# Gate weights of four mLSTM heads folded in four large VectorE instructions, their loads moved earlier, and the heads written one step apart

## The chip, the cores and the metric

The kernel runs on one core of a Trainium2 chip. The metric is the time of one execution on the device in microseconds (us), and each kernel is timed several times. PE is the matmul engine (TensorE), PEld its weight loads, DVE is VectorE, ACT is ScalarE, POOL is GpSimd, and SP is SyncE, which here only issues loads.

## The reference, cut to what matters

Two layers over 256 tokens of 1024 channels: an mLSTM block (4 heads of 512 channels), then a sparse attention block. The change lies in the first part of the mLSTM block.

```
x_in, z = split(rmsnorm(x, g) @ w_in, 2)            # 256 x 2048 each
x_conv  = silu(conv4(x_in) + conv_b)                # 4 taps along the tokens
q, k    = headwise(x_conv, w_q), headwise(x_conv, w_k)   # 4 x 4 blocks
v       = headwise(x_in, w_v)
gates   = concat([q, k, v]) @ w_if + b_if           # 6144 -> 8
h       = mlstm(q, k, v, input gate, forget gate)   # per head, causal, stabilised
out     = ((layernorm(h) * ln_w + skip * x_conv) * silu(z)) @ w_out
```

Since q, k and v are blockwise products, the gates can be computed from x_conv and x_in with *folded* gate weights, w_q and w_k (and w_v) multiplied into w_if. Folding is a product with a broadcast and a sum over the 4 (or 8) inner rows.

## The kernel before, in words

Weights come from HBM in **units** of 1 MB, each in two halves of 512 KB. `load_unit` (L258) issues a half from SP into one of 4 raw buffers `wr`. ACT rounds it to `wh` (L274). The remainder `wl` is made in one of two ways: DVE subtracts (L280), or ACT writes the negated copy (L277) and POOL issues an accumulating transfer `wl<-wr` that adds the raw half (L278). The list `BY_DMA` says which. `wh` and `wl` have 5 buffers each, and two units are loaded ahead (`LOOK`).

`project_channels` (L402) multiplies one unit with the input: 48 matmuls (L411), 16 k-blocks by channels with three products each (two of `wh`, one of `wl`). By `LAG` the products of `wl` stand 4 steps later, so the last 8 matmuls of a unit need the remainder of its second half. Its result lies in a PSUM bank, `px` (2 buffers) or `acc1` (1), until DVE has scaled it by the row scale `rb1` into `xin` (L438). `rb1` comes from `norm1` (L384): sums of squares, two small matmuls (L388), POOL's power (L325), two matmuls (L378) and a copy (L389).

Units 0 to 7 are x_in of the four heads, two each; 8 to 15 are z; 16 to 23 are the output projection (L694). The loop over heads (L431) does for each head h, in the order of the text: two units; block-diagonal matrices of the head's 4 x 4 blocks by POOL (`bdq`, `bdv`, L398); the head's part of the folded gate weights (`gate_weights`, L461: a product L463 and a sum L464, once for v into the last 8 columns of `bdv`, once for q and k into those of `q`); the convolution `xc` on ACT, POOL and DVE (L476 to L487); Silu (L489); the products with the block-diagonal matrices (v by L504, q by L497) and the scores (L511, L512). The gate weights `wif` (768 KB), the constants `cst` (228 KB) and x itself (1 MB, for the residual) are loaded by SP after the first unit's evacuation: a one-element copy from `rb1` into each tile (L441 to L448) makes those loads wait for it.

The order on each engine is not that of the text. A scheduler places the instructions by its own model of their times; each engine then runs its list in order, and a waiting instruction holds what stands behind it on its engine.

Of the kernel before, what the change touches and what calls it, by code (L numbers as in the profile page):

```python
# [202 lines left out]
def trunk(ctx, tc, a, out, dbg=None):  # L203
# [77 lines left out]
            halves.append((hi, lo))  # L281
        return halves

    plan = [(a["wi1"], i, KT, 256) for i in range(16)] + [(a["wo1"], i, 4, 512) for i in range(8)]
    of_step = {"v": [(a["wi2v"], i, 4, 280) for i in range(4)], "c": [(a["wi2"], i, 4, 512) for i in range(2)]}
    for j, step in enumerate(("k", "q0", "q1")):
        of_step[step] = [(a["wi2k"], i, KT, 256) for i in (2 * j, 2 * j + 1)]
# [140 lines left out]
        GP.memset(t, 0.0)  # L428
    xcs, vs1, scs = [], [], []
    convw = CA("convw").rearrange("p (t c) -> p t c", t=4)  # L430
    for h in range(NH):  # L431
        xin = T([P, 4, S + 3], tag="xin", bufs=2)
        GP.memset(xin[:, :, 0:3], 0.0)
        for u in range(2):
            def evac_x(ps, x_=xin[:, 2 * u:2 * u + 2, 3:], first=(h, u) == (0, 0)):
                if first:
                    norm1()
                V.tensor_tensor(x_, ps, spread(rb1), op=OP.mult)  # L438
            project_channels(a["wi1"], 2 * h + u, evac_x, ("px", "px", "acc1")[(2 * h + u) % 3])
            if (h, u) == (0, 0):  # L440
                V.tensor_copy(cst[:, 0:1], rb1[:, 0:1])  # L441
                nc.sync.dma_start(cst, a["cst"][:, 0:n_res])
                wifs = [T([P, 16, n // 128, 8], tag="zt", bufs=ZT, name="wif") for n in (1024, 512)]
                for t, o_, n in zip(wifs, (0, 1024), (1024, 512)):
                    V.tensor_copy(t[:, 0, 0, 0:1], rb1[:, 0:1])
                    nc.sync.dma_start(t.rearrange("p a b c -> p (a b c)"), a["wif"][:, o_:o_ + n])
                for i in range(2):
                    V.tensor_copy(xt[i][:, 0, 0:1], rb1[:, 0:1])  # L448
                    nc.sync.dma_start(xt[i], a["x"][:, i * 512:(i + 1) * 512].rearrange("(t p) c -> p t c", p=P))
        if h == 0:  # L450

            wqk = CA("wqk").rearrange("p (c i) -> p c i", c=16)
            wv = CA("wv").rearrange("p (c i) -> p c i", c=16)
            atmp = T([P, 16, 4, 4], tag="f4", bufs=F4, name="atmp")
            V.tensor_tensor(atmp, CA("wkrep").rearrange("p (c i j) -> p c i j", c=16, i=4),
                            wqk[:, :, 0:4, None].to_broadcast([P, 16, 4, 4]), op=OP.mult)
            AT = T([P, 16, 4], name="AT")
            V.tensor_reduce(AT, atmp.rearrange("p c i j -> p c j i"), axis=AX.X, op=OP.add)
        own = slice(4 * h, 4 * h + 4)

        def gate_weights(out, wgt, wif, nq):  # L461
            tmp = T([P, 4, nq * 4, 8], tag="wtmp", bufs=2)
            V.tensor_tensor(tmp, wif[:, own, :, :], wgt[:, own, :, None].to_broadcast([P, 4, nq * 4, 8]), op=OP.mult)  # L463
            V.tensor_reduce(out, tmp.rearrange("p c i g -> p c g i"), axis=AX.X, op=OP.add)  # L464

        bdq = blockdiag(AT[:, own, :], F32)
        bdv = blockdiag(wv[:, 4 * h:4 * h + 4, :], F32, PG)
        gate_weights(bdv[:, :, P:PG], wv, wifs[1], 1)
        xc = T([P, 4, S], tag="f4", bufs=F4, name="xc")
        tap_w = lambda tap, c: convw[:, tap, 4 * h + c:4 * h + c + 1]  # L470
        if h in CB_:
            x1 = T([P, 4, S], tag=XT, bufs={"zt": ZT, "sc2": 1}[XT], name="x1")
        for c in range(4):
            cbias = CA("convb")[:, 4 * h + c:4 * h + c + 1]
            if h in CA_ or h in CB_:
                A.activation(xc[:, c, :], xin[:, c, 0:S], AF.Identity, scale=tap_w(0, c), bias=cbias)  # L476
            else:
                V.tensor_scalar(xc[:, c, :], xin[:, c, 0:S], tap_w(0, c), cbias, op0=OP.mult, op1=OP.add)
            if h in CB_:
# [12 lines left out]
        gate_weights(q[:, :, S:SG], wqk, wifs[0], 2)
        for c2 in range(2):
            ps = PS((P, 2, S))
            for c in range(2):
                k = 2 * c2 + c
                PE.matmul(ps[:, c, :], bdq[:, k, :], xc[:, k, :], start=True, stop=True)  # L497
            A.activation(q[:, 2 * c2:2 * c2 + 2, 0:S], ps, AF.Copy)
        v = T([P, 2, 4, PG], tag="f4", bufs=F4, name="v")
        rest = PS((P, 2, PG), tag="acc0")  # L500
        for tb in range(2):
            ps = PS((P, 3, PG), tag="pt")
            for c in range(4):
# [12 lines left out]
        V.tensor_tensor(gsc, gsc, ps[:, P:P + 2 * PG].rearrange("p (t n) -> p t n", t=2)[:, :, P:PG], op=OP.add)  # L516
        xcs.append(xc)
        vs1.append(v)
        scs.append(sc)

    ident_r = TS([P, P], F32R, name="ident_r")
    V.tensor_copy(ident_r, ident)
    maskt_r = T([P, 2, P], F32R, name="maskt_r")
    V.tensor_copy(maskt_r, C("maskt")[:, None, :].to_broadcast([P, 2, P]))
    causal = C("mask2")

    vsps = []
# [116 lines left out]
    lnw = CA("lnw")  # L644
    ys = []
    for h in range(NH):
        z = T([P, 4, S], tag="zt", bufs=ZT, name="z")
        for u in range(2):
# [72 lines left out]
    def after_block(n, tb, cols):  # L721
        squares(ss2, n, tb)

    nc.sync.dma_start(pkb, a["pkb"])
    gain2 = CB("g")

    def before_unit(n, kq):
# [416 lines left out]
```

## Time and profile before

| | |
|---|---|
| median of 3 runs | 381.38 us (380.86 to 384.1) |
| the profiled execution | 378.87 us, of which its span 377.1 us |
| mean granted PE clock | 0.984 |
| busy in the span | PE 350.6, DVE 255.7, ACT 241.5, POOL 134.7 us |

The span is from the first to the last instruction; 1.8 us lie around it. Busy times of engines overlap. PE is busy nearly throughout, so what PE waits for, and where, is what counts.

### The profile page before, as it was taken

What the parts mean: (1) busy time and instruction counts of PE and PEld (TensorE: products, weight loads), DVE (VectorE), ACT (ScalarE), POOL (GpSimd) and SP (SyncE); (2) the same over time, 40 slices, a digit from 0 to 9 for tenths busy, and PEclk for the clock granted to TensorE, in tenths of its full rate; (3) what the DMA queues carried; (4) which work ended last, traced back from release to release, by engine and by line L of the source; (5) the groups of instructions that cost most, each with busy time, mean ns of one, the idle gap of its engine ahead of it and who ended that gap; (6) DMA issues with size and microseconds to landing.
All of it is one profiled execution on the core that took longest, in us unless ns stands there. A gap on an engine that the chain in (4) does not pass through costs nothing.

```text
span 377.1 us, 6621 instructions
## 1 busy us (share of the span) xinstructions
PE 350.6 (93%) x2399; PEld 313.8 (83%) x2399; DVE 255.7 (68%) x535; ACT 241.5 (64%) x438; POOL 134.7 (36%) x165
## 2 busy tenths in 40 slices
PE   6998799979999979999999799999879999999991
PEld 6998799869998968988887699999869996777771
DVE  5976999756476548983243736687979789684515
ACT  6674669738468649765653744372579789996304
POOL 5226377433301124610100303283430283857003
PEclk9999899999999999999999999999989999999997
DMA  7889758765646978999998897546577865020003
GB/s 260 280 269 315 209 129 217 188 152 125 167 157 159 197 210 217 228 233 296 239 262 239 266 343 216 173 104 155 154 195 209 246 237 158 2 56 2 2 0 112
DMA packets 21633, 69.57 MB, mean 185 GB/s; under 512 B 2528, under 2 KB 2912, under 8 KB 21600
## 3 DMA queue, kind: packets, MB, share of 16 engines
q1 hardware_dynamic: 15472, 48.71, 38.7%
q0 software_dynamic: 4752, 16.83, 24.6%
q10 hardware_dynamic: 1376, 3.61, 2.9%
q8 instruction: 19, 0.31, 0.3%
q14 instruction: 14, 0.11, 0.1%
HBM read 50.87 MB, written 1.05 MB: 138 GB/s over the span
## 4 chain that ended last, share of the span: by engine, by line
PE 39%; DMA 23%; DVE 18%; issue 8%; ACT 8%; POOL 1%; SPq 1%; ACTq 0%; POOLq 0%; DVEq 0%
PE ps L411 17%; DMA wl<-wr 7%; DMA wr<-in_wo_dram 6%; DVE xc L487 6%; PE ps L694 6%; DVE wl L280 4%; DMA wr<-in_wi2z_dram 3%; DMA wr<-in_wi2k_dram 2%; ACT wh L274 2%; PE ps L984 2%; PE ps L909 2%; PE ps L897 2%; DMA cst<-in_cst_dram 2%; DMA xch<-in_xt_dram 1%; ACT wl L277 1%
## 5 line engine op out<-in xcount | busy, mean ns | idle before, releaser
L411 PE MATMUL ps<-hT,wh 128*128 128x256 f32 x832 | 139.5, 293 | 2.4 <-DVE hT L343 1.3
L274 ACT ACTIVATE wh<-wr 128x1024 fp32r<-128x1024 f32 (+2 forms) x90 | 89.5, 1000 | 58.1 <-PE ps L411 21.5
L411 PEld LDWEIGHTS ps<-hT,wh 128*128 128x128 f32 x832 | 121.8, 198 | 4.6 <-DVE hT L343 1.9
L280 DVE TENSOR_TENSOR wl<-wr,wh 128x1024 fp32r<-128x1024 f32 (+2 forms) x57 | 70.9, 1244 | 36.0 <-ACT wh L274 33.2
L411 PE MATMUL ps<-hT,wl 128*128 128x256 f32 x416 | 87.7, 287 | 0.0
L411 PEld LDWEIGHTS ps<-hT,wl 128*128 128x128 f32 x416 | 66.4, 193 | 1.0 <-issue 0.6
L278 POOL DMA_DIRECT2D wl<-wr x33 | 28.7, 877 | 107.9 <-ACT wl L277 103.5
L277 ACT ACTIVATE wl<-wr 128x1024 fp32r<-128x1024 f32 (+1 forms) x33 | 33.8, 1025 | 13.4 <-PE ps L694 6.6
L694 PE MATMUL ps<-wh,r 128*128 128x512 f32 x128 | 41.4, 398 | 0.0
L487 DVE SCALAR_TENSOR_TENSOR xc<-xin,pka,xc 128x256 f32<-128x256 f32 x44 | 30.8, 754 | 0.1
L694 PEld LDWEIGHTS ps<-wh,r 128*128 128x128 f32 x128 | 24.0, 188 | 5.5
L694 PE MATMUL ps<-wl,r 128*128 128x512 f32 x64 | 25.3, 395 | 0.0
L694 PE MATMUL ps<-wh,y 128*128 128x512 f32 x64 | 21.8, 406 | 0.0
L803 POOL TENSOR_TENSOR swap<-swap,trig 128x512 f32<-128x512 f32 x6 | 10.2, 1697 | 18.9 <-DMA swap<-qu 7.3
L775 PE MATMUL ps<-wl,hT 128*128 128x280 f32 (+1 forms) x48 | 15.8, 330 | 1.2 <-DMA wl<-wr 1.2
L846 PE MATMUL ps<-ka,qt 128*128 128x256 f32 (+1 forms) x32 | 12.0, 380 | 3.8 <-DVE nm L852 3.7
L774 PE MATMUL ps<-wh,hT 128*128 128x280 f32 (+1 forms) x48 | 15.5, 329 | 0.0
L776 PE MATMUL ps<-wh,hT 128*128 128x280 f32 (+1 forms) x48 | 15.2, 325 | 0.0
L694 PEld LDWEIGHTS ps<-wh,y 128*128 128x128 f32 x64 | 11.8, 188 | 3.1 <-issue 0.8
L694 PEld LDWEIGHTS ps<-wl,r 128*128 128x128 f32 x64 | 12.0, 188 | 2.8 <-DMA wl<-wr 0.2
L641 POOL TENSOR_TENSOR xc<-xc,pka 128x1024 f32<-128x1024 f32 x4 | 9.8, 2455 | 12.2 <-PE ps L512 12.2
L504 PE MATMUL ps<-m,xin 128*128 128x136 f32 x64 | 9.7, 299 | 3.6 <-DVE m L464 3.5
(473 smaller groups left out, 676.0 us busy)
## 6 DMA issues: line engine op xcount, KB each, us to landing
wr<-in_wi_dram SPq DMA_DIRECT2D x34, 512.0 KB
wl<-wr POOLq DMA_DIRECT2D x31, 512.0 KB, 5.9
wr<-in_wo_dram SPq DMA_DIRECT2D x24, 512.0 KB
wr<-in_wi2k_dram SPq DMA_DIRECT2D x12, 512.0 KB
wr<-in_wi2z_dram SPq DMA_DIRECT2D x8, 512.0 KB
wr<-in_wi2v_dram SPq DMA_DIRECT2D x8, 280.0 KB
cw<-in_cw_dram ACTq DMA_DIRECT2D x4, 512.0 KB
xch<-in_xt_dram SPq DMA_DIRECT2D x4, 256.0 KB
```

The costliest lines, as they stand in the source:

```text
L274: A.activation(hi[:, k, :], raw[:, k, :], AF.Copy)
L277: A.activation(lo[:, k, :], raw[:, k, :], AF.Copy, scale=-1.0)
L278: GP.dma_start(out=lo[:, k, :].rearrange("p k n -> p (k n)"), in_=raw[:, k, :].rearrange("p k n -> p (k n)"), accum_op=OP.add)
L280: V.tensor_tensor(lo[:, k, :], raw[:, k, :], f32(hi[:, k, :]), op=OP.subtract)
L411: PE.matmul(ps[:, c, :], w, (hl if i == 1 else hh)[:, k, :], start=(k, c, i) == (0, 0, 0), stop=(k, i) == (KT - 1, 2), skip_group_check=True)
L487: V.scalar_tensor_tensor(xc[:, c, :], xin[:, c, tap:tap + S], tap_w(tap, c), xc[:, c, :], op0=OP.mult, op1=OP.add)
L694: PE.matmul(acc, l, r[:, k % 2, cols], start=first and i == 0, stop=last and i == 2)
L774: PE.matmul(o_, lh, hi[:, k % 2, :], start=kt == 0, stop=False)
L775: PE.matmul(o_, lh, lo[:, k % 2, :], start=False, stop=False)
L776: PE.matmul(o_, ll, hi[:, k % 2, :], start=False, stop=kt == KT - 1)
L803: (GP, V)[RE[1]].tensor_tensor(sw, sw, turn(1), op=OP.mult)
L846: PE.matmul(o_, lq, ka[:, g, :, 0:w_], start=True, stop=False)
```

## The change

- The loads of `cst` and `wif` wait for the sum of squares (`sq1`) and no longer for `rb1`; the load of x and of `pkb` (140 KB, before it was among the first loads) waits for the first evacuation of head 2 (`XTH`).
- The folding for all heads is done once (`fold`): two products (128x512 and 128x1024) and two sums, in place of eight products and eight sums. For each head POOL copies 128x32 out of the result into `bdv` and `q`.
- The text of the head loop is split in two, `heads_x` (units) and `heads_products` (the rest), and written in the order A0 A1 B0 A2 B1 A3 B2 B3.
- Two casts, `ident_r` and `maskt_r`, go from DVE to POOL.
- `silu_z1` and the stages "Z" are written down and not used.

```diff
+    def heads_x(h):
+        xin = xins[h] = T([P, 4, S + 3], tag="xin", bufs=2)
...
             project_channels(a["wi1"], 2 * h + u, evac_x, ("px", "px", "acc1")[(2 * h + u) % 3])
             if (h, u) == (0, 0):
-                V.tensor_copy(cst[:, 0:1], rb1[:, 0:1])
-                nc.sync.dma_start(cst, a["cst"][:, 0:n_res])
...
+                small_weights()
+        if h == XTH:
+            V.tensor_copy(pkb[:, 0:1], xin[:, 0, 3:4])
+            nc.sync.dma_start(pkb, a["pkb"])
...
+    def small_weights():
+        wifs = [T([P, 16, n // 128, 8], tag="zt", bufs=ZT, name="wif") for n in (1024, 512)]
+        V.tensor_copy(cst[:, 0:1], sq1[:, 0, 0:1])
+        for t, o_, n in zip(wifs, (0, 1024), (1024, 512)):
+            V.tensor_copy(t[:, 0, 0, 0:1], sq1[:, 0, 0:1])
+            nc.sync.dma_start(t.rearrange("p a b c -> p (a b c)"), a["wif"][:, o_:o_ + n])
+        nc.sync.dma_start(cst, a["cst"][:, 0:n_res])
...
+        def gate_weights(wgt, wif, nq, name):
+            out = T([P, 16, 8], name=name)
+            tmp = T([P, 16, nq * 4, 8], tag="f4", bufs=F4, name="wtmp")
+            V.tensor_tensor(tmp, wif, wgt[:, :, :, None].to_broadcast([P, 16, nq * 4, 8]), op=OP.mult)
+            V.tensor_reduce(out, tmp.rearrange("p c i g -> p c g i"), axis=AX.X, op=OP.add)
+            return out
+        folded.update(AT=AT, wv=wv, gv=gate_weights(wv, wifs[1], 1, "gwv"), gq=gate_weights(wqk, wifs[0], 2, "gwq"))
...
-        gate_weights(bdv[:, :, P:PG], wv, wifs[1], 1)
+        GP.tensor_copy(bdv[:, :, P:PG], folded["gv"][:, own, :])
...
-        gate_weights(q[:, :, S:SG], wqk, wifs[0], 2)
+        GP.tensor_copy(q[:, :, S:SG], folded["gq"][:, own, :])
...
+    for stage in STAGES.split():
+        {"A": heads_x, "B": heads_products, "Z": silu_z1}[stage[0]](int(stage[1]))
+
     ident_r = TS([P, P], F32R, name="ident_r")
-    V.tensor_copy(ident_r, ident)
+    GP.tensor_copy(ident_r, ident)
     maskt_r = T([P, 2, P], F32R, name="maskt_r")
-    V.tensor_copy(maskt_r, C("maskt")[:, None, :].to_broadcast([P, 2, P]))
+    GP.tensor_copy(maskt_r, C("maskt")[:, None, :].to_broadcast([P, 2, P]))
```

What the scheduler makes of it stands at three places. First **DVE**, before, from the third evacuation on (`ps_402` is unit 2, `xc_325` head 0, `m` a block-diagonal matrix):

```order
L438 TENSOR_TENSOR xin_387<-ps_402,rb_29_153 128x2x256
L524 CAST maskt_r_971<-cst_70 128x256
L487 SCALAR_TENSOR_TENSOR xc_325<-xin_159,pka_71,xc_325 128x256 x4
L463 TENSOR_TENSOR wtmp_322<-wif_242,pka_71 128x128
L463 TENSOR_TENSOR wtmp_347<-wif_241,pka_71 128x256
L464 TENSOR_REDUCE m_58_320<-wtmp_322 128x4x8
L464 TENSOR_REDUCE q_346<-wtmp_347 128x4x8
L280 TENSOR_TENSOR wl_454<-wr_452,wh_453 128x1024
```

and now, from the last remainder ahead of the row scale (`ps_173`, `ps_260`, `ps_325` are units 0, 1, 2; L394 is the copy into `rb1`, L481 and L482 the large products and sums, L445 the evacuation):

```order
L285 TENSOR_TENSOR wl_314<-wr_312,wh_313 128x1024
L394 COPY rb_29_153<-ps_231 128x256
L481 TENSOR_TENSOR wtmp_443<-wif_240,pka_71 128x512
L481 TENSOR_TENSOR wtmp_447<-wif_239,pka_71 128x1024
L395 TENSOR_SCALAR rb1h_154<-rb_29_153 128x256
L445 TENSOR_TENSOR xin_159<-ps_173,rb_29_153 128x2x256
L445 TENSOR_TENSOR xin_159<-ps_260,rb_29_153 128x2x256
L482 TENSOR_REDUCE gwv_442<-wtmp_443 128x128
L445 TENSOR_TENSOR xin_310<-ps_325,rb_29_153 128x2x256
L482 TENSOR_REDUCE gwq_446<-wtmp_447 128x128
```

The large products now stand between the copy of the row scale and the first evacuation; before, they stood behind three evacuations.

Second **POOL**, before, from the power of the row scale on (`wl_259` is the second half of unit 3):

```order
L325 TENSOR_TENSOR r_43_228<-r1me_226,mhalf_88 128x2
L278 DMA wl_259<-wr_257 128x1024
L482 TENSOR_TENSOR xc_325<-xc_325,x_61_326 128x512
L398 TENSOR_TENSOR m_57_318<-AT_316,cst_70 128x512
L398 TENSOR_TENSOR m_58_320<-pka_71,cst_70 128x4x128
L398 TENSOR_TENSOR m_87_515<-AT_316,cst_70 128x512
L398 TENSOR_TENSOR m_88_517<-pka_71,cst_70 128x4x128
L398 TENSOR_TENSOR m_116_709<-AT_316,cst_70 128x512
```

and now (`wl_255` is the second half of unit 3, `wl_320` of unit 4):

```order
L330 TENSOR_TENSOR r_43_228<-r1me_226,mhalf_88 128x2
L403 TENSOR_TENSOR m_76_450<-AT_440,cst_70 128x512
L403 TENSOR_TENSOR m_77_452<-pka_71,cst_70 128x4x128
L403 TENSOR_TENSOR m_104_649<-AT_440,cst_70 128x512
L403 TENSOR_TENSOR m_105_651<-pka_71,cst_70 128x4x128
L403 TENSOR_TENSOR m_131_839<-AT_440,cst_70 128x512
L562 CAST maskt_r_965<-cst_70 128x256
L283 DMA wl_255<-wr_253 128x1024
L283 DMA wl_320<-wr_318 128x1024
L494 COPY m_77_452<-gwv_442 128x4x8
L494 COPY m_105_651<-gwv_442 128x4x8
```

The accumulating transfer of unit 3 stood right behind the power and ahead of all block-diagonal matrices; now five of those and a cast stand ahead of it.

Third **PE**, before, where head 0's products of v stand (`ps_596` is unit 4):

```order
L411 MATMUL ps_596<-hT_126,wh_390 128x256
L504 MATMUL ps_360<-m_58_320,xin_159 128x136 x3
L504 MATMUL ps_359<-m_58_320,xin_159 128x136
L504 MATMUL ps_366<-m_58_320,xin_159 128x136 x3
L504 MATMUL ps_359<-m_58_320,xin_159 128x136
L411 MATMUL ps_596<-hT_125,wh_390 128x256
```

and now (`ps_388` is unit 3, `ps_530` unit 4):

```order
L416 MATMUL ps_388<-hT_125,wl_249 128x256
L530 MATMUL ps_488<-m_77_452,xin_159 128x136 x2
L416 MATMUL ps_388<-hT_125,wl_255 128x256 x8
L530 MATMUL ps_488<-m_77_452,xin_159 128x136
L530 MATMUL ps_487<-m_77_452,xin_159 128x136
L530 MATMUL ps_494<-m_77_452,xin_159 128x136 x3
L530 MATMUL ps_487<-m_77_452,xin_159 128x136
L416 MATMUL ps_530<-hT_125,wh_313 128x256
```

They stood after 14 matmuls of unit 4 and now stand around the last 8 of unit 3, which read `wl_255`. Elsewhere on PE, the two matmuls for the sum of squares stand after 43 matmuls of unit 1 (before: after 6), and the two that spread the row scale (L383, before L378) after 32 of unit 2 (before: after 10).

## Rows read from the trace of the kernel before

**Rows 1.** The page: busy times, and the chain that ended last by engine.

```profile
PE 350.6 (93%) x2399; PEld 313.8 (83%) x2399; DVE 255.7 (68%) x535; ACT 241.5 (64%) x438; POOL 134.7 (36%) x165
...
PE 39%; DMA 23%; DVE 18%; issue 8%; ACT 8%; POOL 1%; SPq 1%; ACTq 0%; POOLq 0%; DVEq 0%
```

**Rows 2.** What PE waited for, whole span: us, times, longest us.

```profile
PE ps L504 <- DVE m L464: 3.5, 1, 3.5
PE ps L497 <- DVE gsc L516: 2.4, 1, 2.4
PE ps L615 <- ACT hn L639: 2.3, 1, 2.3
...
PE ps L775 <- DMA wl<-wr: 1.2, 1, 1.2
```

**Rows 3.** Timeline, 18 to 43 us: PE's rows, POOL's power, the copy of rb.

```profile
18.51 1.63 POOL L325 TENSOR_TENSOR r<-r1me,mhalf 128x2 f32<-128x2 f32 x1 [7.01 <-DVE r1me L323]
...
23.88 0.61 PE L378 MATMUL ps<-dg,onesq 128*128 128x128 f32 x4
...
24.53 0.42 DVE L389 COPY rb<-ps 128x256 f32<-128x256 f32 x1 [1.37 <-PE ps L378]
...
28.88 2.32 PE L411 MATMUL ps<-hT,wh 128*128 128x256 f32 x18
...
34.64 1.84 PE L411 MATMUL ps<-hT,wh 128*128 128x256 f32 x14
39.97 2.88 PE L504 MATMUL ps<-m,xin 128*128 128x136 f32 x16 [3.49 <-DVE m L464]
```

**Rows 4.** Stretches of time: busy us of each engine, then clock, DMA share, GB/s.

```profile
20.00:36.50 16.50, 16.48 (x138) 16.28 (x136) 11.35 (x20) 10.66 (x15) 6.85 (x7) 1.00 0.93 287
...
40.00:44.50 4.50, 4.50 (x25) 4.50 (x26) 4.50 (x9) 3.34 (x6) 1.11 (x2) 0.62 0.89 194
...
160.00:206.00 46.00, 46.00 (x208) 37.22 (x207) 21.80 (x27) 26.83 (x33) 6.00 (x7) 1.00 0.98 252
```

**Rows 5.** Timeline of DVE from 25 us.

```profile
25.20 0.68 DVE L438 TENSOR_TENSOR xin<-ps,rb 128x512 f32<-128x512 f32 x1
...
26.70 1.22 DVE L280 TENSOR_TENSOR wl<-wr,wh 128x1024 fp32r<-128x1024 f32 x1
...
32.04 0.29 DVE L524 CAST maskt_r<-cst 128x256 fp32r<-128x256 f32 x1 [2.26 <-DMA cst<-in_cst_dram]
32.25 4.83 DVE L487 SCALAR_TENSOR_TENSOR xc<-xin,pka,xc 128x256 f32<-128x256 f32 x4
37.00 2.53 DVE L463 TENSOR_TENSOR wtmp<-wif,pka 128x128 f32<-128x128 f32 x2
...
41.39 0.62 DVE L463 TENSOR_TENSOR wtmp<-wif,pka 128x128 f32<-128x128 f32 x2
...
73.40 5.20 DVE L487 SCALAR_TENSOR_TENSOR xc<-xin,pka,xc 128x256 f32<-128x256 f32 x1
```

**Rows 6.** Timeline of POOL: first and last of five L398, then 73 us.

```profile
32.15 1.09 POOL L398 TENSOR_TENSOR m<-AT,cst 128x512 f32<-128x512 f32 x1 [2.95 <-DMA cst<-in_cst_dram]
...
36.76 1.23 POOL L398 TENSOR_TENSOR m<-AT,cst 128x512 f32<-128x512 f32 x1
...
73.78 2.20 POOL L641 TENSOR_TENSOR xc<-xc,pka 128x1024 f32<-128x1024 f32 x1
75.64 2.66 POOL L534 TENSOR_TENSOR vsp<-v,vsp 128x1024 fp32r<-128x1024 f32 x1
```

**Rows 7.** The chain that ended last, 25 us: start, us, what.

```profile
25.97 6.04 DMA cst<-in_cst_dram
```

**Rows 8.** The line L278: its 33 accumulating transfers, issue to landing.

```profile
DMA to landing us min/median/max: 3.8/5.8/10.8
```

**Rows 9.** Timeline of ACT, 137 to 141 us.

```profile
137.33 1.06 ACT L274 ACTIVATE wh<-wr 128x1024 fp32r<-128x1024 f32 x1 [5.59 <-DMA wr<-in_wo_dram]
...
140.94 1.45 ACT L639 ACTIVATE hn<-ps,nb,s 128x512 f32<-128x512 f32 x2 [0.24 <-POOL nb L636]
```

More of the change, by code (lines that the diff above doesn't have):

```diff
@@ L67 @@
 XT = 'zt'
+XTH = 2
 NOT_POOL = (0, 1, 2, 11)
@@ L70 @@
 BY_DMA = [(i, 1) for i in list(range(24)) + list(range(24, 48, 2)) if i not in NOT_POOL] + [(i, 0) for i in BOTH]
+WI1 = range(16)
+STAGES = "A0 A1 B0 A2 B1 A3 B2 B3"
 _C = {}
@@ L282, in load_unit @@
         return halves
-    plan = [(a["wi1"], i, KT, 256) for i in range(16)] + [(a["wo1"], i, 4, 512) for i in range(8)]
+    plan = [(a["wi1"], i, KT, 256) for i in WI1] + [(a["wo1"], i, 4, 512) for i in range(8)]
     of_step = {"v": [(a["wi2v"], i, 4, 280) for i in range(4)], "c": [(a["wi2"], i, 4, 512) for i in range(2)]}
@@ L430, in trunk @@
     convw = CA("convw").rearrange("p (t c) -> p t c", t=4)
-    for h in range(NH):
-        xin = T([P, 4, S + 3], tag="xin", bufs=2)
+    xins, zt_ = {}, {}
+    def heads_x(h):
+        xin = xins[h] = T([P, 4, S + 3], tag="xin", bufs=2)
         GP.memset(xin[:, :, 0:3], 0.0)
@@ L440, in trunk @@
             if (h, u) == (0, 0):
-                V.tensor_copy(cst[:, 0:1], rb1[:, 0:1])
-                nc.sync.dma_start(cst, a["cst"][:, 0:n_res])
[L443 to L449, printed above, removed]
@@ L450, in trunk @@
-        if h == 0:
[L452 to L458, printed above, removed]
@@ L459, in trunk @@
-        own = slice(4 * h, 4 * h + 4)
[L461 to L467, printed above, removed]
-        gate_weights(bdv[:, :, P:PG], wv, wifs[1], 1)
+                small_weights()
@@ new lines, in heads_x @@
+        if h == XTH:
+            V.tensor_copy(pkb[:, 0:1], xin[:, 0, 3:4])
+            nc.sync.dma_start(pkb, a["pkb"])
+            for i in range(2):
+                V.tensor_copy(xt[i][:, 0, 0:1], xin[:, 0, 3:4])
+                nc.sync.dma_start(xt[i], a["x"][:, i * 512:(i + 1) * 512].rearrange("(t p) c -> p t c", p=P))
+    folded = {}
+    def small_weights():
[5 more added lines that the diff above has]
+        nc.sync.dma_start(cst, a["cst"][:, 0:n_res])
+        folded["wif"] = wifs
@@ new lines, in fold @@
+    def fold():
+        wifs = folded["wif"]
+        wqk = CA("wqk").rearrange("p (c i) -> p c i", c=16)
+        wv = CA("wv").rearrange("p (c i) -> p c i", c=16)
+        atmp = T([P, 16, 4, 4], tag="f4", bufs=F4, name="atmp")
+        V.tensor_tensor(atmp, CA("wkrep").rearrange("p (c i j) -> p c i j", c=16, i=4),
+                        wqk[:, :, 0:4, None].to_broadcast([P, 16, 4, 4]), op=OP.mult)
+        AT = T([P, 16, 4], name="AT")
+        V.tensor_reduce(AT, atmp.rearrange("p c i j -> p c j i"), axis=AX.X, op=OP.add)
+        def gate_weights(wgt, wif, nq, name):
[5 more added lines that the diff above has]
+        folded.update(AT=AT, wv=wv, gv=gate_weights(wv, wifs[1], 1, "gwv"), gq=gate_weights(wqk, wifs[0], 2, "gwq"))
@@ L469, in trunk, with heads_products @@
+    def heads_products(h):
+        if h == 0:
+            fold()
+        xin = xins.pop(h)
+        own = slice(4 * h, 4 * h + 4)
+        bdq = blockdiag(folded["AT"][:, own, :], F32)
+        bdv = blockdiag(folded["wv"][:, own, :], F32, PG)
+        GP.tensor_copy(bdv[:, :, P:PG], folded["gv"][:, own, :])
         xc = T([P, 4, S], tag="f4", bufs=F4, name="xc")
@@ L519, in trunk, with silu_z1, evac_z @@
         scs.append(sc)
+    def silu_z1(h):
+        z = zt_[h] = T([P, 4, S], name="z")
+        for u in range(2):
+            def evac_z(ps, z=z[:, 2 * u:2 * u + 2, :]):
+                V.tensor_tensor(z, ps, spread(rb1), op=OP.mult)
+                A.activation(z, z, AF.Silu)
+            project_channels(a["wi1"], 8 + 2 * h + u, evac_z)
+    for stage in STAGES.split():
+        {"A": heads_x, "B": heads_products, "Z": silu_z1}[stage[0]](int(stage[1]))
     ident_r = TS([P, P], F32R, name="ident_r")
-    V.tensor_copy(ident_r, ident)
+    GP.tensor_copy(ident_r, ident)
     maskt_r = T([P, 2, P], F32R, name="maskt_r")
-    V.tensor_copy(maskt_r, C("maskt")[:, None, :].to_broadcast([P, 2, P]))
+    GP.tensor_copy(maskt_r, C("maskt")[:, None, :].to_broadcast([P, 2, P]))
     causal = C("mask2")
@@ L646, in trunk @@
     for h in range(NH):
-        z = T([P, 4, S], tag="zt", bufs=ZT, name="z")
-        for u in range(2):
+        z = zt_[h] if h in zt_ else T([P, 4, S], tag="zt", bufs=ZT, name="z")
+        for u in range(0 if h in zt_ else 2):
             def evac_z(ps, z=z[:, 2 * u:2 * u + 2, :]):
@@ L722, in after_block @@
         squares(ss2, n, tb)
-    nc.sync.dma_start(pkb, a["pkb"])
     gain2 = CB("g")
```

## The prediction

> **What bounds the kernel now.** I read the page first: PE is busy in 93% of the span, no other engine in more than 68%, and the chain that ended last is of PE in 39%, of DMA in 23% and of DVE in 18% [rows 1]. So the time is PE's work, which the change leaves as it is, plus PE's waits. The list of PE's waits has two in the first part, where the change lies: 3.5 us until a sum of gate weights (L464) and 2.4 us under a name of DVE (L516), and later 2.3 us until a hn of ACT and 1.2 us until an accumulating transfer [rows 2].
>
> Then the timeline, for the cause of the first. PE had done 14 matmuls of unit 4 at 36.5 us and sat still to 39.97 [rows 3]. DVE stood at the cast maskt_r, idle until cst had landed at 32.0, 6.04 us after its issue at 25.97 [rows 5, 7]. Behind that cast stood four taps of the convolution, 4.83 us, and two products of gate weights, 2.53 us, while POOL ran block-diagonal matrices back to back from 32.15 [rows 5, 6]; the same pair of products took 0.62 at 41.39 [rows 5]. After the wait PE was also slow: from 40.0 to 44.5 the granted clock averaged 0.62 [rows 4], so part of it ran at the lower of its two levels, half speed. That is (1 - 0.62) x 4.5 = 1.7 us of work lost.
>
> The second wait has another cause. At 73.40 one tap of the convolution of head 2 took 5.20 us on DVE while POOL ran 2.20 and 2.66 us of other work [rows 5, 6], and PE waited for the products of that head behind it.
>
> **What goes.** The loads of cst and wif no longer wait for rb1. In the new order on SP they stand behind the second half of unit 3 and the first of unit 4. The one-element copies that release wif stand on DVE right behind the remainder of unit 2's first half. That remainder followed the instruction that released POOL's power at 18.51 [rows 3] and takes 1.22 [rows 5], so wif is issued about 20. With 6.04 us to land, as cst under a similar load (DMA share 0.93, [rows 4, 7]), it lands near 26.4. The cast maskt_r is off DVE, so nothing of DVE waits for cst, and PE's row of head 0's products moves with the rest. I take the 3.5 us and the 1.7 us of slow clock as gone. The second wait, 2.4, goes as a place: head 2's taps stand elsewhere. Together 7.6 us.
>
> DVE also loses work: of eight products and eight sums four remain, larger ones. That counts only through these waits. The copies of gate weights for each head are small instructions on POOL, behind the first products; they delay head 0's products of v only if they come later than 40 matmuls of unit 3, about 36 us, and the first large sum is long done then. I cost them at nothing; without that cover head 0's products wait as they did before, up to 3.5 us [rows 2]. The load of x and pkb moves from the crowded stretch at 26 to 37 us to about 50; it is not read before the output projection, and behind it SP has loads for unit 8, which PE reaches some 20 us later. Nothing; without that margin 1.19 MB at the 287 GB/s of rows 4 would cost 4.1 us.
>
> **What comes, term by term.**
>
> *Unit 3 waits for px.* Unit 3 needs the bank of unit 0, so the first evacuation. It began at 28.88 [rows 3], and units 0 to 2 are the same work. Before, that evacuation stood at 25.20 [rows 5], 3.7 us early. Now the two matmuls that spread the row scale stand 22 matmuls later in unit 2. A unit is 48 matmuls from 28.88 to 34.64, 0.12 us each [rows 3], so this is 2.6 us. The copy rb moves from 24.53 to 27.1 and ends at 27.5. Behind it now stand the two large products, 1536 elements per partition. By the remainder of 1024, 1.22 us [rows 5], that is 1.85. With rb1h (under the 0.42 of the copy of the same size, [rows 3]; I take 0.3) and the evacuation itself (0.68) the bank is free at 30.3 when nothing disturbs them, and PE waits 1.4 us. But POOL runs its five block-diagonal matrices then: the power ends 4.4 us later than before, since its matmuls stand 37 later in unit 1, so at 24.5 instead of 20.14 [rows 3], and five of 1.2 [rows 6] last to 30.5. The disturbed pair lost 2.53 - 0.62 = 1.9 us [rows 5], which would make the wait 3.3. I take 1.0 for it, because POOL is near its end when the second product starts: **2.4 us**, bounds 1.4 and 3.3.
>
> Here the profile shows DVE's products and taps stretched where POOL works [rows 5, 6]. The Trainium skill ("SBUF — State Buffer", Who interferes with whom) states the reason: a VectorE instruction with two SBUF inputs contends with a GpSimd instruction that reads SBUF, whichever starts first holds the shared port for its whole length, and a reduction never contends. Rows 5 agree in kind (2.53 against 0.62). By the rule each of two products waits for one POOL instruction at most, 2 x 1.2, and the wait would be 3.8, the sum 1.4 less gain than by mine. It also speaks against moving casts and copies to POOL at just this place.
>
> *The last 8 matmuls of unit 3 wait for wl.* The accumulating transfer of that half stood right behind the power. Now five L398 and a cast of half their size (0.6) stand ahead of it, so POOL issues it near 31.1. Landing takes 3.8, 5.8 or 10.8 us [rows 8]: 34.9, 36.9 or 41.9. PE wants it 40 matmuls and two small ones after 31.3, at 36.3. So 0, **0.6** or 5.6 us.
>
> *Taps against POOL once more.* The skip product (L641) and the remainder of v on POOL still fall beside taps of a later head; by the order it is head 3's. Before this cost 2.4 us once [rows 2]. The products of q of head 3 now stand after 34 matmuls of unit 8, some 4 us of cover. From 0 to 2.7; I take **1.3**.
>
> *Behind the head loop.* The 2.3 us wait for hn [rows 2]: ACT held at a weight half of the output projection, 5.59 us until its load, with hn behind it [rows 9]. In the new order two hn of ACT stand ahead of that row, so the wait should go. But from 160 to 206 the DMA share is 0.98 [rows 4], and PE's wait of 1.2 us for a transfer [rows 2] comes at the end of that stretch. Where PE comes earlier to that stretch than the loads do, it waits there instead. I count half, **1.15** gained, between 0 and 2.3. What is gained before 115 us keeps, as I read it, since the loads are released by PE's progress through the buffers and move with it.
>
> **The sum.** -7.6 - 1.15 + 2.4 + 0.6 + 1.3 = -4.45 us. The profiled execution would be 378.87 - 4.45 = 374.4. It lies 2.5 us under the median of the runs, and I take the same difference for the median: **376.9 us**, or 1.2% faster. About 1%, 3.8 us, is what a measurement of this kernel can tell from no change.
>
> **The rivals.**
>
> 1. *DVE's queue becomes the bound at unit 3* (no change). If wif lands near 30 instead of 26.4, the large products wait for it, with three evacuations behind them. PE then waits about 4.9 instead of 2.4, as long as before, and the clock falls again (1.7). New costs: 4.9 + 1.7 + 0.6 + 1.3 = 8.5, against 8.75 gone. The median stays near 381. For it: one landing of 6.04 us is all I have, and seven loads of 512 KB are in flight around it. Against it: it needs only 27.5.
> 2. *The late accumulating transfer* (slower). If it lands at the upper bound, 41.9, PE waits 5.6 in the midst of unit 3, the clock falls (1.7), and the raw buffer that it frees comes late for unit 6, for which I put half a unit, 2.9. 2.4 + 5.6 + 1.7 + 2.9 + 1.3 = 13.9, less 8.75: 5.2 slower, 386.5. It decides from a landing of about 40, 9 us after issue; the median transfer took 5.8 [rows 8].
> 3. *Everything goes and little comes* (faster). The products find POOL's gaps (1.4), no other wait, the hn wait gone for good: -7.6 - 2.3 + 1.4 = -8.5, 372.9.
> 4. *Given back to the loads.* The loop of raw buffers at DMA share 0.98 from 160 to 206 [rows 4] does not move with PE, and the gain turns into waits at the end of that stretch: at most 1 us stays, 380.4. Against it: ahead of 115 us the DMA engines have spare time, and in the long stretch ACT's rows wait for PE as well as for loads.
>
> **How the numbers follow.** Forecast 0.52, rival 1 0.15, rival 2 0.09, rival 3 0.15, rival 4 0.09. The forecast's own range, with the bounds of its terms, is 374.0 to 379.5, and some three fifths of it lie under 377.6. Faster by over 1%: 0.31 + 0.15 + a little of the rest = 0.50; slower 0.09; same 0.41. The range 372.4 to 381.5 leaves out rival 2 and the ends of rivals 1 and 3.
>
> **What would show it.** After the change: no wait of PE at 36 to 40 us and no half-clock stretch behind it; a new wait of PE on xin L445 at about 29 us, 1.4 to 3.3; the large products at 27.5, longer than 1.85 together; wif landed before them; unit 3's last products close behind wl; no wait for hn; the wait for a transfer near 200 us larger than 1.2. I am wrong if the new wait at 29 is over 4.5, if the clock falls again there, or if the part behind 115 us takes longer than before.

## The result, and the profile after

| | before | after |
|---|---|---|
| median of 4 runs each, same chip | 381.12 us (379.45 to 384.1) | 394.14 us (388.77 to 398.35) |
| the profiled execution, its span | 378.87, 377.1 us | 394.88, 393.1 us |

The changed kernel is slower: ratio 1.034, 95% interval 1.025 to 1.042. By the ratio that is 12.8 us more, where 4.5 less was forecast. Ratios here and below leave out executions more than 1.5% above the fastest of the same kernel, so they can differ from the quotient of the medians shown.

The page of the changed kernel, the parts that answer to [rows 1]: busy times, then the chain that ended last by engine.

```profile
PE 359.6 (91%) x2399; PEld 318.4 (81%) x2399; DVE 256.6 (65%) x522; ACT 242.3 (62%) x438; POOL 140.5 (36%) x175
...
PE 56%; DVE 14%; DMA 14%; ACT 6%; issue 6%; POOL 1%; SPq 1%; ACTq 1%; POOLq 0%; DVEq 0%
```

PE has the same 2399 instructions and is busy 9 us longer. The list of what PE waited for after the change, which answers to [rows 2] (us, times, longest us):

```profile
PE ps L416 <- DVE xin L445: 3.7, 1, 3.7
PE ps L732 <- DMA wl<-wr: 3.5, 4, 1.5
PE ps L883 <- DVE nm L889: 2.8, 1, 2.8
PE ps L537 <- DVE gsc L542: 2.1, 1, 2.1
...
PE ps L811 <- ACT hT L347: 1.5, 1, 1.5
PE ps L523 <- ACT xc L515: 1.3, 1, 1.3
PE ps L1044 <- DVE kcb L1038: 1.3, 1, 1.3
PE ps L416 <- DVE z L966: 1.2, 1, 1.2
...
PE ps L416 <- DVE z L690: 1.2, 1, 1.2
...
PE ps L812 <- DMA wl<-wr: 0.8, 1, 0.8
```

The waits for a sum of gate weights and for hn are gone. Against them stand the forecast wait for xin (3.7), gsc once more (2.1), xc (1.3), and a handful behind the head loop: 3.5 and 0.8 us for accumulating transfers, where [rows 2] has 1.2 us at L775, and hT, kcb and two z. Next DVE and POOL around 25 us, start and length in us, to set beside [rows 5] and [rows 6]. First DVE:

```profile
25.50 2.07 DVE L382 TENSOR_SCALAR dg<-pk,r 128x128 f32<-128x128 f32 x2 [0.61 <-POOL r L330]
27.49 2.08 DVE L285 TENSOR_TENSOR wl<-wr,wh 128x1024 fp32r<-128x1024 f32 x1
29.50 0.41 DVE L394 COPY rb<-ps 128x256 f32<-128x256 f32 x1
29.83 3.19 DVE L481 TENSOR_TENSOR wtmp<-wif,pka 128x512 f32<-128x512 f32 x2
32.94 0.48 DVE L395 TENSOR_SCALAR rb1h<-rb 128x256 f32<-128x256 f32 x1
33.34 1.27 DVE L445 TENSOR_TENSOR xin<-ps,rb 128x512 f32<-128x512 f32 x2
```

and POOL at the same time:

```profile
27.45 1.04 POOL L403 TENSOR_TENSOR m<-AT,cst 128x512 f32<-128x512 f32 x1
28.45 2.03 POOL L403 TENSOR_TENSOR m<-pka,cst 128x512 f32<-128x512 f32 x1
30.44 1.49 POOL L403 TENSOR_TENSOR m<-AT,cst 128x512 f32<-128x512 f32 x1
31.88 1.39 POOL L562 CAST maskt_r<-cst 128x256 fp32r<-128x256 f32 x1
```

From 25.50 on DVE is never idle here, so wif had landed when the products began. Rows on both engines are stretched: a remainder takes 2.08 us where [rows 5] has 1.22, and a block-diagonal matrix 2.03 where the one ahead of it took 1.04. The two rows dg, from which the row scale is spread, take 2.07; before, they took 0.48:

```profile
20.17 0.48 DVE L377 TENSOR_SCALAR dg<-pk,r 128x128 f32<-128x128 f32 x2 [0.61 <-POOL r L325]
```

Stretches of time after (columns as in [rows 4]):

```profile
33.70:37.00 3.30, 2.84 (x13) 2.87 (x14) 3.30 (x5) 2.95 (x7) 1.87 (x4) 0.50 0.75 141
...
67.90:71.10 3.20, 3.20 (x12) 2.79 (x12) 2.42 (x5) 1.88 (x2) 0.00 (x0) 0.50 0.71 209
221.50:224.70 3.20, 3.20 (x9) 2.43 (x9) 3.17 (x8) 2.23 (x6) 0.00 (x0) 0.50 1.00 291
286.40:293.00 6.60, 5.60 (x23) 5.34 (x23) 3.69 (x14) 4.72 (x14) 0.88 (x1) 0.50 0.88 265
...
120.00:160.00 40.00, 40.00 (x293) 37.21 (x292) 30.49 (x83) 30.03 (x43) 15.27 (x20) 1.00 0.72 181
```

PE ran at half clock right behind the wait for xin, as it had behind the old one, and in three more stretches. Without one at the very end, which both kernels have, the four are 17 us long by the clock's records. Before there were two, from 41.1 to 44.5 and from 276.6 to 280.0, 7 us together. 10 us more at half clock are 5 us of work lost, some half of PE's 9 us. The last row becomes the key: in the same 40 us before, the loads moved more.

```profile
120.00:160.00 40.00, 37.70 (x258) 33.91 (x257) 27.30 (x79) 28.64 (x42) 14.10 (x21) 1.00 0.86 211
```

Unit 9 ended 4.5 us later than before (107.86 against 103.36); the end lay 16 us later. So most of the loss is made behind the head loop, where the diff changes no work but the place of the load of pkb. The scheduler had ordered that part anew: of the 1710 PE instructions behind the loop at most 1353 stand in the same order among each other in both kernels, of ACT's 280 only 206, of DVE's 360 only 249.

### The profile page after: what moved, and what is told of

The parts are those of the page before. It is cut to its first block, busy times and chain, and to the rows that moved or that the text cites. A ratio compares the mean times of both kernels' runs of the same rounds, so it can differ in the third digit from the quotient of the medians.

```text
span 393.1 us, 6633 instructions
## 1 busy us (share of the span) xinstructions
PE 359.6 (91%) x2399; PEld 318.4 (81%) x2399; DVE 256.6 (65%) x522; ACT 242.3 (62%) x438; POOL 140.5 (36%) x175
## 4 chain that ended last, share of the span: by engine, by line
PE 56%; DVE 14%; DMA 14%; ACT 6%; issue 6%; POOL 1%; SPq 1%; ACTq 1%; POOLq 0%; DVEq 0%
PE ps L416 25%; PE ps L732 7%; DMA wl<-wr 5%; DVE xc L513 5%; DMA wr<-in_wo_dram 4%; DVE wl L285 2%; PE ps L946 2%; PE ps L653 2%; PE ps L934 2%; PE ps L1021 2%; DMA wr<-in_wi_dram 2%; ACT wh L279 2%; PE ps L537 2%; ACT wl L282 2%; PE ps L883 1%
## 5 line engine op out<-in xcount | busy, mean ns | idle before, releaser
L416 PE MATMUL ps<-hT,wl 128*128 128x256 f32 x416 | 89.2, 288 | 0.0
L416 PEld LDWEIGHTS ps<-hT,wl 128*128 128x128 f32 x416 | 67.2, 194 | 1.4 <-issue 1.0
L732 PE MATMUL ps<-wh,r 128*128 128x512 f32 x128 | 41.1, 397 | 0.2 <-DVE x L754 0.2
L513 DVE SCALAR_TENSOR_TENSOR xc<-xin,pka,xc 128x256 f32<-128x256 f32 x44 | 29.8, 739 | 4.0 <-ACT xc L502 2.2
L811 PE MATMUL ps<-wh,hT 128*128 128x280 f32 (+1 forms) x48 | 16.9, 363 | 2.0 <-ACT hT L347 1.5
L812 PE MATMUL ps<-wl,hT 128*128 128x280 f32 (+1 forms) x48 | 17.6, 369 | 0.8 <-DMA wl<-wr 0.8
L813 PE MATMUL ps<-wh,hT 128*128 128x280 f32 (+1 forms) x48 | 16.6, 355 | 0.0
L840 POOL TENSOR_TENSOR swap<-swap,trig 128x512 f32<-128x512 f32 x6 | 9.3, 1553 | 15.1 <-DMA swap<-kraw 12.8
L537 PE MATMUL ps<-q,xc 128*128 128x264 f32 x32 | 10.8, 423 | 2.7 <-DVE gsc L542 2.1
```

The costliest lines, as they stand in the source:

```text
L416: PE.matmul(ps[:, c, :], w, (hl if i == 1 else hh)[:, k, :], start=(k, c, i) == (0, 0, 0), stop=(k, i) == (KT - 1, 2), skip_group_check=True)
L732: PE.matmul(acc, l, r[:, k % 2, cols], start=first and i == 0, stop=last and i == 2)
L811: PE.matmul(o_, lh, hi[:, k % 2, :], start=kt == 0, stop=False)
L812: PE.matmul(o_, lh, lo[:, k % 2, :], start=False, stop=False)
L813: PE.matmul(o_, ll, hi[:, k % 2, :], start=False, stop=kt == KT - 1)
```

## The experiments

Order can be held: with order-only dependencies between neighbours of a list, each engine issues that list in order, and nothing else is changed. "Held" below means this, for everything behind the head loop. Ratios are to the kernel before, run in the same session, with 95% intervals.

### Which part of the program: e1, e2

```diff
@@ e1: the changed kernel
+    pin_tail(nc, tc)      # behind the head loop: the order of the kernel before
@@ e2: the kernel before
+    pin_tail(nc, tc)      # behind the head loop: the order of the changed kernel
```

> The changed head loop, and behind it every engine's instructions issued in the order that they have in the kernel before. Theory A (the order that the scheduler gives the rest of the program is what costs most; the head loop itself costs some 3 to 4.5 us): 384 to 386, that is 3 to 5 us over the kernel before, and PE waits in the output projection and behind it as in the kernel before. Theory B (the head loop makes loads and casts late, and the lateness is carried on whatever the order): 389 to 394, as the changed kernel.

> The converse: the head loop of the kernel before, and behind it the order of the changed kernel. Theory A: 386 to 391, slower by 5 to 10 us although nothing of the change itself is in it. Theory B: 379 to 382, no change.

e1 took 380.1 us, ratio 1.002 (0.998 to 1.006); e2 389.4, 1.030 (1.022 to 1.038). So the order behind the loop costs 11.2 us, on a head loop in which nothing was changed: theory A, whose range for e2 holds. e1 lies below both ranges, since the head loop alone costs not 3 to 4.5 us but nothing that can be told from zero. What PE waited for in e1:

```profile
PE ps L416 <- DVE xin L445: 3.7, 1, 3.7
PE ps L537 <- DVE gsc L542: 2.1, 1, 2.1
PE ps L523 <- ACT xc L515: 1.7, 1, 1.7
```

and the same 40 us of e1 and then of e2:

```profile
120.00:160.00 40.00, 40.00 (x275) 36.14 (x275) 29.39 (x82) 30.19 (x44) 14.53 (x21) 1.00 0.88 216
```

```profile
120.00:160.00 40.00, 40.00 (x283) 37.03 (x282) 31.59 (x84) 28.99 (x40) 15.21 (x20) 1.00 0.76 178
```

With before's order 216 GB/s, with the other one 178, though PE is busy throughout in both. Behind 160 us the loads have little room to catch up (DMA share 0.98 before, [rows 4], and 0.92 in e2), and e2 waits there:

```profile
PE ps L695 <- DMA wl<-wr: 5.0, 3, 2.5
```

### Which part of the change draws the other order: e3, e12, e14

```diff
@@ e3: the changed kernel, held to the order before
-STAGES = "A0 A1 B0 A2 B1 A3 B2 B3"
+STAGES = "A0 B0 A1 B1 A2 B2 A3 B3"
@@ e12: the kernel before, its head loop split in heads_x and heads_products
+STAGES = "A0 A1 B0 A2 B1 A3 B2 B3"
@@ e14: e12
+    pin_tail(nc, tc)      # the order of the kernel before
```

> The changed kernel without its staggering: the heads' two parts in turn (A0 B0 A1 B1 ...), everything else of the change kept, and the rest in the order of the kernel before. If the large products ahead of the first evacuation are the loss of the head loop, the wait of PE on xin at 30 us stays at 3 to 4 us and the time is that of the first run of this set within 1 us. If the heads one step apart are the loss (PE's wait for the sum gsc at 65 us, 2.1 us, and the half clock behind it, 1.7), this run is 3 to 4 us faster than the first.

> The kernel before of which only the heads are set one step apart (A0 A1 B0 A2 ...): small gate weights for each head, all loads and casts as before, and the rest in the order that the scheduler gives it. Theory (the staggering alone turns the scheduler's order behind the head loop into the slow one; with the heads in turn the changed kernel has the order of before there): 386 to 394. Rival (the slow order needs the other parts of the change too): 378 to 382.

> The twelfth run (staggered heads alone, 397 us) with the rest in the order of the kernel before. Theory (nearly all of its 17 us is the order behind the head loop): 379 to 384. Rival (the staggered head loop with late loads and small gate weights is itself slow): 388 to 396.

Without the staggering (e3) the scheduler's own order behind the loop is before's, so that holding it alters nothing (e13 below, heads in turn and not held, has the same order in its trace). e3 took 378.93, ratio 1.000 (0.996 to 1.005), by the ratios 0.6 us under e1, so the staggering costs the head loop nothing that can be told from zero. Its waits show the price of the large products:

```profile
PE ps L416 <- DVE xin L445: 3.7, 1, 3.7
...
PE ps L530 <- DVE xin L445: 2.8, 1, 2.8
```

Staggering alone (e12) took 396.48, the median of three, ratio 1.048 (1.039 to 1.057); a fourth execution of 864.74 us, which is also the one profiled, is left out of both, and so no row of e12 is read. With before's order behind it (e14) 381.53 are left, 1.006 (1.001 to 1.010). So of its 4.8% some 4.2 are the order behind the loop, no less than in e2 (3.0), and the staggering gains nothing within it. The staggering by itself leads to a slow order.

### The head loop: e4, e8, e5, e10, e13, e11

```diff
@@ e4: the kernel before, held to its order; e8: the same, not held
-                V.tensor_copy(cst[:, 0:1], rb1[:, 0:1])
+                V.tensor_copy(cst[:, 0:1], sq1[:, 0, 0:1])
...
-                    V.tensor_copy(t[:, 0, 0, 0:1], rb1[:, 0:1])
+                    V.tensor_copy(t[:, 0, 0, 0:1], sq1[:, 0, 0:1])
@@ e5: e1, and e13: e3, not held
+        with tc.issue_after(evacs[1]):     # DVE: behind the second evacuation
             folded.update(AT=AT, wv=wv, gv=gate_weights(wv, wifs[1], 1, "gwv"), ...
@@ e10: e5
+        with tc.issue_after(gscs[h - 2]) if h >= 2 else nullcontext():   # DVE: the taps
@@ e11: e4
+        with tc.issue_after(evacs[3]) if h == 1 else nullcontext():      # DVE: the taps
```

> The kernel before, of which only the release of the loads of cst and wif is changed (by the sums of squares and not by the row scale), the rest in its own order. Theory (the wait of 3.5 us at 36 us is the late landing of cst, and the clock falls for it): that wait and the half clock behind it (1.7) go, 375 to 377. Rival (the same engine is late there for another reason, its taps and products beside POOL): the wait shrinks by 1 to 2 us only and the time is 379 to 381.

> The kernel before with only the earlier release of the loads of cst and wif, and the rest in whatever order the scheduler now gives it (the fourth run had the order of before and took 374.7 us). Theory (any edit of the head loop makes the scheduler draw another order behind it, and that is worth as much as the edit): the time differs from 374.7 by more than 1%, 379 to 390. Rival (only the staggered heads lead to the slow order): 373 to 376.5.

The earlier loads alone took 374.67 (0.987, 0.979 to 0.995) and 374.88 (0.986, 0.981 to 0.991). That is the whole gain that any version had. e8 also came out in before's order of its own accord: not every edit draws another one, as I had supposed. PE's wait for m is gone, and the next on DVE's queue is late in its place (e4), with half clock behind it from 48.8 to 52.2 us:

```profile
PE ps L504 <- DVE xin L438: 3.1, 1, 3.1
```

So the time came out about where the theory had it, but not by the wait and the clock that it named: 3.1 us and half clock again stand where 3.5 us and half clock stood. What is missing in the lists of e4 and e8 are the waits for gsc at L497 (2.4) and for hn (2.3) of [rows 2]. That these make the gain is not shown: other waits changed as well, and the executions profiled (378.49 and 377.38 us) lie above the medians.

> The changed head loop, with the large products and sums of gate weights issued on DVE behind the first two evacuations of xin and not ahead of them; the rest in the order of the kernel before. Theory (unit 3 of the projection waits only because the large products, 3.2 us, stand ahead of the evacuation that frees its bank): that wait falls from 3.7 to under 1 us, the half clock behind it (1.7) goes, and the time is 374 to 376.5 against some 380 of the first run. Rival (the head's products then wait for the sums instead): a new wait of 2 to 3 us on DVE or POOL at 36 to 42 us, 377.5 to 380.

> The fifth run (changed head loop, folding behind the first evacuations, rest as before) with the sums gsc of the head two back issued on DVE ahead of a head's taps. Theory (at 64 us PE waits 2.4 us because that sum stands behind eight taps that POOL's products stretch to 6.5 us, and the clock falls for it, 1.7): 375 to 377. Rival (the taps then end later and PE waits for xc instead): 378.5 to 380.

> The change without its staggering (heads in turn) and with the large products behind the first two evacuations of xin; the scheduler's own order behind the head loop, which then is that of the kernel before. Theory (of the third run, 378.9 us, PE's wait for xin at 30 us, 3.7, and the half clock behind it, 1.7, go, and one new wait of 1 to 2 us for the sums or taps comes): 374 to 376.5, as the early loads alone. Rival (what unit 3 gains is lost at the head's products, as in the fifth run): 378 to 380.

e5 took 379.38 (0.997, 0.992 to 1.003): the wait for xin fell from 3.7 to 0.9 and the half clock behind it went, but the time stayed. That is the rival's time, but not its place: the head's products waited for no sum of gate weights. Two other waits grew, with half clock behind them from 66.3 to 69.7 us:

```profile
PE ps L524 <- ACT xc L516: 2.9, 2, 1.7
PE ps L538 <- DVE gsc L543: 2.4, 1, 2.4
```

The second one's cause stands in e5's timeline of DVE, where gsc needs 0.16 us and stood behind eight taps:

```profile
59.89 6.50 DVE L514 SCALAR_TENSOR_TENSOR xc<-xin,pka,xc 128x256 f32<-128x256 f32 x8 [0.61 <-ACT xc L503]
66.31 0.16 DVE L543 TENSOR_TENSOR gsc<-gsc,ps 128x16 f32<-128x16 f32 x1
66.39 1.27 DVE L514 SCALAR_TENSOR_TENSOR xc<-xin,pka,xc 128x256 f32<-128x256 f32 x3
```

With gsc ahead of those taps (e10) that wait went, and the time came to 375.46, 0.993 (0.988 to 0.998); by the ratios that is 1.6 us less than e5, with intervals that overlap. e13 puts the large products behind the evacuations, as e5 does, for the heads in turn and without holding anything; gsc it leaves in its place. It took 375.55, 0.987 (0.978 to 0.997), and most of what is left in its head loop is

```profile
PE ps L416 <- DVE xin L445: 1.9, 1, 1.9
...
PE ps L524 <- DVE gsc L543: 1.3, 1, 1.3
```

> The fourth run (kernel before with the earlier loads of cst and wif, 374.7 us) with the taps of head 1 issued on DVE behind the evacuation of that head's second half. Theory (PE's wait of 3.1 us for that xin at 45 us is DVE's queue, where two taps beside POOL took 4.6 us ahead of it, and the clock falls behind it, 1.7): the wait goes and the time is 370 to 372. Rival (the head's products wait for xc instead, since its taps end later): 373.5 to 375.5.

e11 is inconclusive: 375.57 (370.97 to 379.23), with no interval for its ratio. The wait for xin went, but 3.3 us for accumulating transfers came, and with them half clock:

```profile
49.00:54.00 5.00, 5.00 (x25) 5.00 (x25) 5.00 (x11) 2.97 (x6) 1.11 (x2) 0.50 0.96 308
```

### Inside the other order: e6, e7, e9, e15

```diff
@@ e6: the kernel before
+    pin_tail(nc, tc)      # layer 1 in the order of the changed kernel, layer 2 as before
@@ e7: the kernel before
+    pin_tail(nc, tc)      # the converse
@@ e9: e6, order of ACT (and the transfer of that cast on POOL)
+      wl (L277)
       hn of head 2 (L640)
-      wl (L277)
@@ e15: e9, order of PE
+      the last ten products of unit 13 (L411)
       attention products of head 2 (L616)
-      the last ten products of unit 13 (L411)
```

> The head loop of the kernel before; behind it the instructions of the first layer (attention, gates z, output projection) issued in the order of the changed kernel, those of the second layer in the order of the kernel before. If the two layers' orders cost independently, as the traces have it (5 us more by the end of the first output projection, 6 more behind it): 383 to 385.5. If the loss of the second layer is only the lateness of the first carried on: 388 to 391 here and no loss in the converse.

> The converse: the first layer in the order of the kernel before, the second in that of the changed kernel. Independent costs: 383 to 386. Loss carried on from the first layer: 378 to 380.

e6 took 383.94, ratio 1.014 (1.008 to 1.020), and e7 387.64, 1.018 (1.010 to 1.026). Together they make e2's 1.030 within the intervals: two losses that add up, neither carried on from the other. Layer 1's is in the loads of 120 to 160 us, first e6, then e7:

```profile
120.00:160.00 40.00, 40.00 (x285) 37.00 (x284) 31.49 (x86) 29.54 (x41) 15.21 (x20) 1.00 0.76 177
```

```profile
120.00:160.00 40.00, 40.00 (x282) 36.24 (x281) 28.50 (x82) 31.10 (x46) 13.46 (x20) 1.00 0.88 206
```

Against before's 211 GB/s e6 is 34 short, 1.36 MB in 40 us. At the 255 that e6 reached from 160 to 206 us that is an estimated 5.3 us, and e6 lost 5.4. In that stretch the scheduler had moved casts of weights behind work on heads. One place, ACT in e6:

```profile
138.67 1.05 ACT L277 ACTIVATE wl<-wr 128x1024 fp32r<-128x1024 f32 x1
142.18 1.45 ACT L640 ACTIVATE hn<-ps,nb,s 128x512 f32<-128x512 f32 x2 [2.46 <-POOL nb L637]
143.52 1.05 ACT L277 ACTIVATE wl<-wr 128x1024 fp32r<-128x1024 f32 x1
```

Before, both casts of this line stood ahead of the hn of all heads, of which head 0's began at 140.94 [rows 9]:

```profile
139.66 1.04 ACT L277 ACTIVATE wl<-wr 128x1024 fp32r<-128x1024 f32 x1
```

Here heads 0 and 1 are done by then, and the second cast waits behind the hn of head 2, which waits for POOL: it began 3.9 us later. The fifth load of the output projection's weights, issued at 147.44 us before, is issued at 152.11.

> The sixth run (first layer in the order of the changed kernel, second in that of the kernel before) with one move: on ACT the weight cast wl of the second half of the first unit of the output projection stands ahead of the two hn of head 2 and not behind them, and on POOL its accumulating transfer ahead of the three small instructions of that head. Theory (ACT idles 2.5 us for nb there, the raw buffer behind that transfer comes free 4 us later than before, and the loads of the output projection stay late by that much: PE's three waits for wl, 3.7 us, and half a clock stretch, 1.7): 379 to 381.5 instead of 384. Rival (many rows of the order cost a little each, and this one is made good by the next): 383 to 385.

> The kernel with layer 1 in the changed kernel's order and one weight cast of ACT put ahead of hn of head 2 (382.6 us, ratio 1.012), with one more move, on PE: the last ten products of the 13th unit stand ahead of the attention products of head 2 instead of behind them. Nothing is left out. Theory (PE's order holds the weight buffers): the cast that waited 2.97 us for a free remainder buffer waits under 1, the loads behind it are issued some 2 us earlier, hn comes no later, and the time falls to 379 to 381 us, ratio about 1.003. Rival (the attention products are late then and hn with them, and what was gained at the first pass of the output projection is given back at the second, where the loads are saturated): 382 to 384 us, ratio 1.010 or more.

e9 took 382.57, 1.012 (1.004 to 1.020), which can't be told from e6. That fifth load was issued at 149.81. The first pass of the output projection ended 3.0 us earlier than in e6, the second only 0.2: behind the first PE waited for DVE to evacuate it, and ran at half clock from 183.6 to 187.0.

```profile
PE ps L695 <- DVE x L717: 2.0, 1, 2.0
```

The cast itself had found another hindrance, PE, which still held the buffer that it writes:

```profile
142.02 1.06 ACT L277 ACTIVATE wl<-wr 128x1024 fp32r<-128x1024 f32 x1 [2.97 <-PE ps L411]
```

In e15 PE's order was mended for the unit that held it, and both casts ran in one go:

```profile
138.50 2.00 ACT L277 ACTIVATE wl<-wr 128x1024 fp32r<-128x1024 f32 x2
```

The fifth load was issued at 147.39 us, as early as before, but the sixth at 156.9 against 154.9. The loads of 120 to 160 us in e15, then in e9:

```profile
120.00:160.00 40.00, 40.00 (x285) 36.99 (x284) 31.23 (x86) 29.18 (x41) 14.98 (x20) 1.00 0.78 182
```

```profile
120.00:160.00 40.00, 39.95 (x283) 36.93 (x284) 30.39 (x80) 28.52 (x40) 13.33 (x19) 1.00 0.73 170
```

The first pass of e15 then ended 0.1 us behind before's, but the second 3.2, and the time was 383.47, 1.013 (1.001 to 1.024). The rival was right in what came of it, not in its reason: hn of head 2 came 0.7 us later than in e6 and 3.6 earlier than in e9. One cast in time doesn't bring the bytes back, 182 GB/s are not 211. Nor is the sum of bytes a price: by it e9, with 170 GB/s, should have lost more than e6, and it did not. That the order makes loads late, and that this cast did so for one of them, is shown; which of its other moves do so is not.

## Why the prediction was wrong, point by point

**The step that failed is "Behind the head loop".** I wrote: "What is gained before 115 us keeps, as I read it, since the loads are released by PE's progress through the buffers and move with it", and gave the term bounds of 0 to 2.3 gained. I had seen in the new order that two hn of ACT stood ahead of a cast row, and read that as the end of a wait. It was the sign of another order throughout, and I put no loss on it. e2 measured 11.2 us lost there, e1 that without it the changed kernel is level with before. The wait for hn did go, as forecast, but it is also missing in e1, e3, e4 and e8, which have before's order, so the new order isn't shown to be why. What I called rival 4, a DMA share of 0.98 that turns gains into waits, was the mechanism of layer 1's half of it, but as a loss and not only as a gain given back: a load that the order keeps back before 160 us was not made up behind it. For layer 2's half (e7) the list after the change has the new waits for kcb and z, which e7 has too, and half clock from 286.4 to 293.0; e1, which has before's order there, ran as long at half clock. None of them was tried, so the cause of this half stays open.

**What goes: half right.** The 3.5 us for m went. The 1.7 us of slow clock went from its place and came back behind the wait for xin. The 2.4 us for gsc "goes as a place", I wrote; it came as 2.1 at another head, with 1.3 to 1.7 for xc beside it. I had taken 1.3 for both, bounds 0 to 2.7; 3.4 to 3.8 came.

**Unit 3 waits for px: the mechanism right, the size not.** I put 2.4 between 1.4 and 3.3; 3.7 came. The products took 3.19 and not 2.85. What I had left out stands ahead of the copy: the two rows dg, 2.07 instead of 0.48, and behind them the remainder, 2.08 instead of 1.22. DVE was so late by them that the copy began at 29.50, though the matmuls whose result it copies had ended at 28.5, and it ended 0.9 later against PE than in my sum. I had priced POOL's interference for the products alone. The Trainium skill ("SBUF — State Buffer", Who interferes with whom), by whose rule I had worked out 3.8, has an exclusive lock of the shared port in it, so that POOL's rows stretch as well. The trace agrees in kind: 2.03 and 1.49 us beside 1.04 on POOL, 2.08 beside 1.22 on DVE. That 3.8 is so near to 3.7 is luck: it has the products at 4.25 (1.85 and twice 1.2) and the copy in time.

**The last 8 matmuls of unit 3**: 0.6 forecast, none seen. wl_255 was issued at 33.2, 2.1 us later than forecast, and landed at 38.0. That would have been late for PE at 36.3, as I had it; but unit 3 began 5.3 us later than before and ran in part at half clock, and PE came to that half at 40.7.

**The sum for the head loop** was -7.6 + 2.4 + 0.6 + 1.3 = -3.3. With what e1 shows it is -7.6 + 3.7 + 1.7 + 3.8, and 1.7 for a half-clock stretch at 273.5 to 280.4 that is twice as long as before's, less 2.3 for hn: +1.0. By its ratio e1 is 0.65 slower (-0.9 to 2.2). The forecast's own range, 374.0 to 379.5, is narrower than its bounds add up to: 372.9 to 380.4, even with no more than the 0.6 for wl.

**The rivals.** Rival 1 had the price of the head loop nearly right (no change, and the clock falls again), but not its condition, since wif was there in time: the products were late by the copy, and long, both beside POOL. Rival 2 had the right sign only; its late transfer didn't come. Among the signs of being wrong, "if the clock falls again there" came true, and "if the part behind 115 us takes longer than before" named the place; no chance stood behind it.

## What to carry to other kernels

Where a scheduler orders the engines, an edit's price can be that of a whole new order (e12), or not (e8): compare the orders of the parts that the diff doesn't touch, and where they differ, give that term bounds on both sides of zero. Hold the old order there before judging the edit; here it was the difference between 3.4% slower and no change, and the simplest part, two loads released earlier, was worth 1.4% by itself. A wait that is taken away shows what was next behind it (m, then xin; xin, then gsc and xc), so place short instructions that PE waits for ahead of long ones before counting the gain.

## What the runs showed that I had not expected

Unit 0 is the same work in both kernels, yet it ended at 16.66 us before and at 18.05 after. The stretch 14.0 to 16.4 us of the kernel before:

```profile
14.00:16.40 2.40, 2.40 (x23) 2.40 (x22) 2.37 (x5) 1.12 (x2) 0.00 (x0) 1.00 0.55 169
```

and of the changed one:

```profile
14.00:16.40 2.40, 2.40 (x13) 2.40 (x13) 2.40 (x4) 1.06 (x1) 0.00 (x0) 1.00 0.52 67
```

PE was busy throughout in both, with 23 matmuls and with 13: 0.10 us each against 0.18. The clock's column says 1.00 for both, but the records of the clock begin only at 16.6 us in the changed kernel's profile (13.8 before), so its 1.00 is no reading; in e1 and e4 the column shows 0.50 for 10.0 to 13.5 us. That PE started at half clock for longer in the one execution than in the other fits these times and isn't shown. The difference of start is worth 1.4 us in a single profiled execution, and the 4.5 us by which unit 9 ended later hold it.
